# An encoder layer with three token mixers: pooling copies given a greater advance, one multiplication moved from VectorE to GpSimd

## The chip, the cores and the metric

The kernel runs on one core of one Trainium2 chip. The time is that of the device, in microseconds (us), and the median of several runs is what counts. The core's engines are named as the profile names them: PE (TensorE, matmuls; PEld is its weight load), DVE (VectorE), ACT (ScalarE), POOL (GpSimd) and SP (SyncE, which here issues DMAs). Each has its own instruction stream, works through it in order, and waits for the others through semaphores. Matmul results land in PSUM; POOL doesn't touch PSUM in this kernel.

## The reference, cut to what matters

One layer on 512 positions of width 1024, in float32. An RMS norm, one input projection whose columns go to three token mixers and three gates, the mixers, a gated merge, an output projection with residual, and then a SwiGLU feed-forward part (FFN) of inner width 2816.

```python
h = rms_norm(x, norm_mix)
u_pool, u_lru, q, k, v, g_logits = split(h @ w_in)
gates = sigmoid(g_logits + b_gate)
y_pool = pool_mixer(u_pool, w_pool, pool_scale)      # causal means over 2, 4, 8, 16 positions, minus the token, then a 256x256 map per group
y_lru = rglru_mixer(u_lru, ...)                      # short convolution, gates, linear recurrence
y_sb = stick_breaking_attention(q, k, v)             # 8 heads of 128
merged = sum(gates[i] * (y[i] @ w_branch[i]) for i in range(3))
x = x + merged @ w_out
h2 = rms_norm(x, norm_ffn)
x = x + (silu(h2 @ w_ffn_gate) * (h2 @ w_ffn_up)) @ w_ffn_down
```

The RMS norm divides each position by rms = sqrt(mean(x*x) + eps). The kernel keeps 1/rms of the second norm in a tile rb2.

## The kernel before, in words

Activations lie with channels on the 128 partitions and the 512 positions along the free axis. A float32 matmul is made from three passes: each operand is split into a high part in a shorter format and a low part that is the rest (names ending in hi, h and lo, l), and high x high, low x high and high x low are added in PSUM (L309 to L311 in the helper mm3, L318 in the helper product). So each weight tile costs ACT one copy (the high part) and DVE one subtraction (the low part): L141 and L142 in the first stages, L1439 and L1440 in the FFN. Three buffers hold each kind.

Large matrix products are done block-wise with seven products in place of eight (called 11, 12, S2, S1, S3, S4, 22). These need sums of weight blocks, made by DVE (L1421), and partial results copied out of PSUM by ACT (L1492), since the next product is added into the same PSUM bank.

The program is written for a scheduler. It takes the instructions of the five engines in program order and reorders them by priority and by when their inputs would be there; `tc.high_priority(n)` lets what stands in it count as if it had been written n places earlier. EARLY is 300, AHEAD is 200. The streams that come out are fixed before the kernel runs.

*The pooling stage.* Four groups of 256 channels are projected one after the other (pool_chunk, order 1, 0, 3, 2). Each chunk fills two PSUM tiles out of a pool of three (pmm), so a later chunk or branch can start only when a copy has emptied a tile. evac_u makes that copy on ACT (L977); pool_mean then forms the sliding sums on DVE (L985 to L991), and pool_back multiplies by the group's map (tile pps) and scales (L1004, L1005). In between, the tasks of the attention heads are put in: score sigmoids on ACT (L1086, L1087), a scan and a product on DVE (L1090, L1092). After the four chunks come the branch projections (ps_br), which use the same three PSUM tiles.

*The FFN's direct chunks.* The inner width is worked in eleven chunks of 256. The first two (NDIRECT = 2, "direct") are computed in the ordinary way from h2, the second norm's input without 1/rms, since rb2 isn't there yet when they begin. So their results are multiplied by 1/rms afterwards, on both sides of the SiLU. For each half chunk j, with pg and pu the gate and up products in PSUM:

- L1510 (DVE): sg = pg * rb2, which is the SiLU's argument
- L1511 (ACT): sg = SiLU(sg)
- L1512 (DVE): sg = sg * pu
- L1513 (DVE): act = sg * rb2, since pu also lacked its 1/rms

That makes four of each in all. sg lies in a pool with two buffers ("sq2"): the second chunk's two tiles use the buffers of the first chunk's two, and its L1510 may write them only when L1513 has read them. The remaining nine chunks (function seven) use the seven products, with normalised input (tiles B0...). act of both direct chunks is read again only in the last of them, where the operands of the down projection are split.

On POOL itself there is little arithmetic before: constants, and the power function and a few small multiplications of the query scales (L346 to L350, L819); otherwise it issues DMAs, the FFN's only at the down projection (L1552).

Of the kernel before, what the change touches and what calls it, by code (L numbers as in the profile page):

```python
# [11 lines left out]
AF = mybir.ActivationFunctionType  # L12
ALU = mybir.AluOpType
# [13 lines left out]
EARLY = 300  # L27
# [40 lines left out]
def layer_kernel(ctx: ExitStack, tc: tile.TileContext, x, xt, vecs, w_in, w_qkv7, w_gate7, w_pool, w_rg, w_ig,  # L68
                 w_branch, w_br7, w_out, w_fg, w_fu, w_fd, w_fd7, out):
    nc = tc.nc  # L70
    act = nc.scalar.activation
    dve = nc.vector
# [28 lines left out]
    def in_order(ap, b=H):  # L101
        w = ap.ndim == 3
        if b == H:
            return ap.rearrange("p w (b a) -> p w a b" if w else "p (b a) -> p a b", b=b)
        return ap.rearrange("p (c b a) -> p c a b", a=2, b=b)

    def two(ap, b=H):
        w = ap.ndim == 3
        if b == H:
            return ap.rearrange("p w (a b) -> p w a b" if w else "p (a b) -> p a b", b=b)  # L110
        return ap.rearrange("p (c a b) -> p c a b", a=2, b=b)
# [284 lines left out]
    def chan_chunk(key, rhs, nticks=0, pool=None, pair=False):  # L396
        pss = chunk_psum(key, pool, pair)
        for half in range(2):
            half_chunk(pss if type(pss) is list else [pss[:, j, :] for j in range(2)], key, half, rhs,
                       nticks)  # L400
        return pss
# [37 lines left out]
    with ExitStack() as first:  # L439
# [396 lines left out]
        for t in VKQ:  # L836
            ps = {}
# [50 lines left out]
        for cc in range(2):  # L888
# [14 lines left out]
            for nm in ORDER:  # L903
                ps, half, first_, t, ts_, src, ss = plan[nm]
# [18 lines left out]
    def slot(name, dt=F32, shape=(S,)):  # L923
        return sp.tile([P] + list(shape), dt, tag="s", name=name, bufs=NSP - NLD)
# [14 lines left out]
    with ExitStack() as mix:  # L939
# [34 lines left out]

        def evac_u(ps, name):
            u = slot(name)
            act(two(u), in_order(ps), AF.Copy)  # L977
            return u

        def pool_mean(g, j, u):  # L980
# [33 lines left out]
        def pool_chunk(g):  # L1014
            pss = chan_chunk(("pool", g), hn, 1)
            us = [evac_u(pss[j], f"up{g}{j}") for j in range(2)]
            for j in range(2):
                bg.append(lambda j=j, u=us[j]: pool_mean(g, j, u))
            if g != POOL[0]:
                queue_pool_back(POOL[POOL.index(g) - 1])  # L1020
# [199 lines left out]
    with ExitStack() as third:  # L1220
# [42 lines left out]
        for u, nm in BORDER:  # L1263
# [3 lines left out]
            ps = bank[u, z]  # L1267
# [24 lines left out]
    with ExitStack() as ffn:  # L1292
        gp = ffn.enter_context(tc.tile_pool(name="gp", bufs=GBUFS))

        def g4(shape, name, dt=F32):

            return gp.tile([P] + shape, dt, tag="g", name=name)

        def small(name, bufs=1, tag=None, dt=F32):
            return gp.tile([P, S], dt, tag=tag or name, name=name, bufs=bufs)  # L1300
# [5 lines left out]
        rb2 = small("rb2")  # L1306
# [116 lines left out]
        def make_a(upto):  # L1423
            while made[0] < min(upto, len(steps)):
                c, nm = steps[made[0]]
                made[0] += 1
                if (c, nm) == (NDIRECT, "11"):
                    offs.extend(STEPS)
                while made[1] < min(c + 2, DOWN):
                    load_a(made[1])  # L1430
                    made[1] += 1
                sums_a(c, nm)
                A[c, nm] = split_a(raw[c, nm], f"{c}_{nm}")
# [68 lines left out]
        for c in range(NDIRECT):  # L1502
            pg = chan_chunk(("fg", c), h2, 3, fp)
            pu = chan_chunk(("fu", c), h2, 3, fp)
            if c == NDIRECT - 1:
                make_a(3)
            a = g4([2, S], f"act{c}")
            for j in range(2):
                sg = small(f"sg{c}{j}", 2, "sq2")
                dve.tensor_tensor(two(sg), in_order(pg[j]), two(rb2), ALU.mult)  # L1510
                act(sg, sg, AF.Silu)  # L1511
                dve.tensor_tensor(two(sg), two(sg), in_order(pu[j]), ALU.mult)  # L1512
                dve.tensor_tensor(a[:, j, :], sg, rb2, ALU.mult)  # L1513
            acts.append(a)
        tick(len(bg))
        for c in range(NDIRECT, NF // 2):
# [212 lines left out]
```

## Time and profile before

| | |
|---|---|
| median of 3 runs | 874.85 us (873.82 to 877.39) |
| the profiled execution's own time | 873.78 us |
| its span in the profile | 872.0 us |
| PE busy | 859.1 us, 99% |
| DVE busy | 740.8 us, 85% |
| ACT busy | 525.4 us, 60% |
| POOL busy | 90.8 us, 10% |
| granted PE clock | 1.0 throughout |

Times in the profile count from the span's start. A row of the timeline gives the start, the duration, the engine, the line of the program, the operation, what it writes and reads with the shapes, how many such instructions in a row it merges (x2), and in brackets how long the engine had been idle before it and what it then waited for. With x2 the duration is that of both together; successive instructions of one engine overlap by some 0.1 us, so the distance between starts is the pace. A row of the waits names the waiting engine and line, what it waited for, and then the total, the number of times and the longest, in us.

### The profile page before, as it was taken

The page shows a single profiled execution, that of the slowest core. Times are in us where ns is not written, and L with a number is a line of the kernel's source. Part 1 is how long each engine was busy: PE and PEld are TensorE (multiplying, and loading weights), DVE is VectorE, ACT ScalarE, POOL GpSimd, SP SyncE. Part 2 cuts the span into 40 slices and gives each one's busy share as a digit, 9 for nine tenths or more (in the row PEclk, how much of TensorE's full clock was granted, in tenths as well). Part 3 has the DMA queues.
Part 4 walks back from the last instruction along what each step waited for, and adds up shares of the span by engine and source line. Part 5 has one row for each costly group of instructions (what it writes and reads, how often), then busy time and mean ns, then how long its engine had stood idle before and what let it go on. Part 6 is the DMA issues. An engine that isn't in the chain of part 4 may idle for free.

```text
span 872.0 us, 14269 instructions
## 1 busy us (share of the span) xinstructions
PE 859.1 (99%) x5563; PEld 789.4 (91%) x5563; DVE 740.8 (85%) x958; ACT 525.4 (60%) x730; POOL 90.8 (10%) x130
## 2 busy tenths in 40 slices
PE   9999989999999999999999999999999999999998
PEld 7888878888899888889889998889999999999998
DVE  7899797998787699977988796699998888899974
ACT  6655989556956555565665545464555555755642
POOL 1110002132423101000001200000000000031200
PEclk9999999999999999999999999999999999999999
DMA  9586346798592786744636965345543343797913
GB/s 335 160 298 198 97 161 177 206 330 259 174 287 73 228 255 198 225 122 147 216 98 165 201 177 169 98 134 157 144 123 97 104 116 105 232 245 202 195 40 121
DMA packets 116643, 154.08 MB, mean 177 GB/s; under 512 B 8160, under 2 KB 90080, under 8 KB 116576
## 3 DMA queue, kind: packets, MB, share of 16 engines
q1 hardware_dynamic: 103904, 107.30, 38.6%
q0 software_dynamic: 12528, 45.62, 21.8%
q8 instruction: 43, 0.70, 0.3%
q10 hardware_dynamic: 144, 0.26, 0.1%
q14 instruction: 24, 0.20, 0.1%
HBM read 132.71 MB, written 18.87 MB: 174 GB/s over the span
## 4 chain that ended last, share of the span: by engine, by line
PE 77%; DVE 11%; ACT 6%; DMA 3%; issue 2%; SPq 0%; ACTq 0%; DVEq 0%
PE ps_y L318 10%; PE ps_x L318 8%; PE ps_q L831 7%; PE ps_dy L1648 6%; PE ps_dx L1648 5%; DVE wlo L142 3%; PE ps_br L309 3%; PE ps_br L310 3%; PE ps_br L311 3%; PE ps_bY L1274 2%; PE ps_gate L734 2%; PE ps_gy L318 2%; PE ps_bX L1274 2%; PE ps_gx L318 2%; ACT whi L141 2%
## 5 line engine op out<-in xcount | busy, mean ns | idle before, releaser
L141 ACT ACTIVATE whi<-raw 128x1024 fp32r<-128x1024 f32 x69 | 72.8, 1055 | 77.4 <-PE ps_out L310 16.2
L142 DVE TENSOR_TENSOR wlo<-raw,whi 128x1024 fp32r<-128x1024 f32 x69 | 84.3, 1222 | 21.8 <-ACT whi L141 21.3
L142 DVE TENSOR_TENSOR wlo<-qw,whi 128x1024 fp32r<-128x1024 f32 x48 | 58.5, 1222 | 18.2 <-ACT whi L141 18.0
L141 ACT ACTIVATE whi<-qw 128x1024 fp32r<-128x1024 f32 x48 | 50.5, 1054 | 28.9 <-PE ps_q L831 14.8
L1439 ACT ACTIVATE wh_S<-w_S 128x1024 fp32r<-128x1024 f32 x36 | 38.1, 1062 | 32.9 <-PE ps_y L318 19.5
L1552 POOL DMA_DIRECT2D dw<-in_w_down_dram x20 | 16.9, 862 | 306.6 <-DMA dw<-in_w_down_dram 264.3
L1440 DVE TENSOR_TENSOR wl_S<-w_S,wh_S 128x1024 fp32r<-128x1024 f32 x36 | 43.8, 1221 | 3.8 <-ACT wh_S L1439 3.8
L1439 ACT ACTIVATE wh<-w 128x1024 fp32r<-128x1024 f32 x27 | 28.6, 1058 | 27.3 <-issue 9.1
L1440 DVE TENSOR_TENSOR wl<-w,wh 128x1024 fp32r<-128x1024 f32 x27 | 33.0, 1221 | 8.4 <-ACT wh L1439 8.4
L1439 ACT ACTIVATE whdS<-dw 128x1024 fp32r<-128x1024 f32 x20 | 21.2, 1060 | 20.9 <-PE ps_dy L1648 10.6
L1440 DVE TENSOR_TENSOR wldS<-dw,whdS 128x1024 fp32r<-128x1024 f32 x20 | 24.3, 1222 | 5.3 <-ACT whdS L1439 5.3
L1090 DVE TENSOR_TENSOR_SCAN E<-K,ahead 128x512 f32<-128x512 f32 (+3 forms) x32 | 25.4, 815 | 3.9 <-ACT K L1086 3.9
L311 PE MATMUL ps_gate<-HH,wlo 128*128 128x512 f32 x64 | 24.4, 381 | 2.2 <-DVE wlo L142 2.2
L309 PE MATMUL ps_br<-yHH,whi 128*128 128x512 f32 x64 | 24.6, 385 | 1.4 <-ACT up L977 1.4
L309 PE MATMUL ps_lru<-HH,whi 128*128 128x512 f32 x64 | 24.6, 384 | 0.0
L309 PE MATMUL ps_br<-yph,whi 128*128 128x512 f32 x64 | 24.5, 383 | 0.0
L309 PE MATMUL ps_pool<-HH,whi 128*128 128x512 f32 x64 | 24.5, 383 | 0.0
L309 PE MATMUL ps_gate<-HH,whi 128*128 128x512 f32 x64 | 24.4, 381 | 0.0
L310 PE MATMUL ps_lru<-HL,whi 128*128 128x512 f32 x64 | 24.3, 379 | 0.0
L311 PE MATMUL ps_lru<-HH,wlo 128*128 128x512 f32 x64 | 24.3, 379 | 0.0
L310 PE MATMUL ps_gate<-HL,whi 128*128 128x512 f32 x64 | 24.3, 379 | 0.0
L310 PE MATMUL ps_pool<-HL,whi 128*128 128x512 f32 x64 | 24.3, 379 | 0.0
(737 smaller groups left out, 3445.1 us busy)
## 6 DMA issues: line engine op xcount, KB each, us to landing
raw<-in_w_in_dram SPq DMA_DIRECT2D x31, 512.0 KB, 5.4
qw<-in_w_qkv_dram SPq DMA_DIRECT2D x24, 512.0 KB, 7.1
dw<-in_w_down_dram POOLq DMA_DIRECT2D x20, 512.0 KB, 8.7
w<-in_w_ffn_gate_dram SPq DMA_DIRECT2D x36, 256.0 KB, 3.5
w<-in_w_ffn_up_dram SPq DMA_DIRECT2D x36, 256.0 KB, 4.2
raw<-in_w_branch_dram SPq DMA_DIRECT2D x16, 512.0 KB, 3.8
qw<-in_w_qkv_dram POOLq DMA_DIRECT2D x12, 512.0 KB, 8.0
qd<-r POOLq DMA_DIRECT2D x12, 512.0 KB, 7.6
```

Source lines behind the costliest of these rows:

```text
L141: act(hi, raw, AF.Copy)
L142: dve.tensor_tensor(lo, raw, hi.bitcast(F32), ALU.subtract)
L309: nc.tensor.matmul(ps, lh, rh, start=start, stop=False, skip_group_check=skip)
L310: nc.tensor.matmul(ps, lh, rl, start=False, stop=False, skip_group_check=skip)
L311: nc.tensor.matmul(ps, ll, rh, start=False, stop=stop, skip_group_check=skip)
L318: nc.tensor.matmul(o, a_[a][:, w, k, :], il2(b_[b][:, k, :]), start=first and n == k == 0, stop=last and n == 2 and k == 3, skip_group_che ...
L831: nc.tensor.matmul(ps[:, a, :], b_[:, k, ts_], il(a_[:, kk, :]), start=first and n == k == 0, stop=n == 2 and k == 3, skip_group_check=True)
L1090: dve.tensor_tensor_scan(E[:, c0:c0 + n][:, ::-1], K[:, c0 + 1:c0 + n + 1][:, ::-1], ahead[:, S - n:][:, ::-1], 0.0, ALU.mult, ALU.add)
L1274: nc.tensor.matmul(o, ah[x_][:, w, k, :], il2(b[k][y_]), start=first_ and n == k == 0, stop=n == 2 and k == 3, skip_group_check=True)
L1439: act(h, src, AF.Copy)
L1440: dve.tensor_tensor(l, src, h.bitcast(F32), ALU.subtract)
L1648: nc.tensor.matmul(o, a_[a][:, w, k0 + k, :], il2(b_[b][:, k, :]), start=first and i == k == 0, stop=last and i == 2 and k == nk - 1, skip ...
```

## The change

Two independent edits. evac_u's copy is put under high_priority(EARLY), so that the scheduler treats it as if it stood 300 places earlier. And L1513, the second multiplication by 1/rms of the two direct chunks, is issued on POOL instead of DVE. What is computed stays the same. The new line in evac_u shifts the line numbers after it by one: L1513 of the program before is L1514 in the changed one.

```diff
         def evac_u(ps, name):
             u = slot(name)
-            act(two(u), in_order(ps), AF.Copy)
+            with tc.high_priority(EARLY):
+                act(two(u), in_order(ps), AF.Copy)
             return u
...
                 dve.tensor_tensor(two(sg), in_order(pg[j]), two(rb2), ALU.mult)
                 act(sg, sg, AF.Silu)
                 dve.tensor_tensor(two(sg), two(sg), in_order(pu[j]), ALU.mult)
-                dve.tensor_tensor(a[:, j, :], sg, rb2, ALU.mult)
+                nc.gpsimd.tensor_tensor(a[:, j, :], sg, rb2, ALU.mult)
             acts.append(a)
```

## Prediction

> **What bounds the kernel now.** I read the page first (busy shares, then the chain that ended last), after it who waited for whom on the matrix engine (PE), and then the stretches of the two edits.
>
> ```profile
> span 872.0 us, 14269 instructions
> PE 859.1 (99%) x5563; PEld 789.4 (91%) x5563; DVE 740.8 (85%) x958; ACT 525.4 (60%) x730; POOL 90.8 (10%) x130
> ...
> PE 77%; DVE 11%; ACT 6%; DMA 3%; issue 2%; SPq 0%; ACTq 0%; DVEq 0%
> ...
> PE ps_br L309 <- ACT up L977: 1.4, 1, 1.4
> ...
> PE ps_x L318 <- DVE wl_S L1440: 0.8, 1, 0.8
> ...
> PE ps_x L318 <- ACT wh_S L1439: 0.2, 1, 0.2
> ```
>
> PE is busy for 859.1 of 872.0 us, so nothing off PE can bring more than it takes away from PE's waits. Three waits lie where the change works: 1.4 us for a copy of pooling products (L977), and 0.8 + 0.2 us for weights that VectorE (DVE) and ScalarE (ACT) prepare just after the direct chunks. The other waits are elsewhere.
>
> ```profile
> 580.00:600.00 20.00, 20.00 (x119) 18.23 (x118) 20.00 (x23) 12.13 (x14) 0.00 (x0) 1.00 0.80 211
> 600.00:620.00 20.00, 19.07 (x168) 18.68 (x167) 19.38 (x20) 11.31 (x15) 0.00 (x0) 1.00 0.47 132
> 620.00:640.00 20.00, 20.00 (x181) 20.00 (x180) 18.22 (x17) 11.69 (x14) 0.00 (x0) 1.00 0.38 107
> ```
>
> These are windows (stretch, length, then busy time of PE, weight loads, DVE, ACT and POOL, the granted clock, DMA share, GB/s). The products from 594 on are those of the first chunk computed with seven products (11, 12, S2, S1, S3, S4, 22, here the first to the seventh). Around the direct chunks' end DVE is full (20.00 of 20 us) and PE loses 0.93 us in 600 to 620; by 620 to 640 DVE has caught up and PE is full. The clock is 1.00, so PE's pace is not in question.
>
> **Edit 1, the pooling copies.** A greater priority can only change the order in which ACT is given its work. I compared the instruction streams of both builds: of eight copies, only the second chunk's two move, ahead of one sigmoid (L1087, 384 columns). PE's, DVE's, POOL's and SP's streams are untouched by it.
>
> ```profile
> 315.18 0.59 ACT L1087 ACTIVATE A<-z,qrs 128x384 f32<-128x384 f32 x1
> 315.64 1.10 ACT L977 ACTIVATE up<-ps_pool 128x512 f32<-128x512 f32 x2
> ...
> 316.73 0.69 DVE L1092 TENSOR_TENSOR A<-A,E 128x512 f32<-128x512 f32 x1
> ...
> 350.23 1.11 ACT L977 ACTIVATE up<-ps_pool 128x512 f32<-128x512 f32 x2
> ...
> 350.90 0.48 PE L309 MATMUL ps_br<-yHH,whi 128*128 128x512 f32 x1 [1.45 <-ACT up L977]
> ```
>
> The wait of 1.45 us belongs to the fourth chunk's copies at 350.23, and those stay behind the same instructions. The second chunk's copies come 0.46 us earlier (315.64 - 315.18) and no PE wait hangs on them. The sigmoid starts after the two copies, at 315.18 + 1.10 = 316.28, and ends at 316.87, where DVE's product with A started at 316.73: at most 0.15 us late. What hides that is PE's queue of other matmuls: the view of waits names no wait of PE for this product. Uncovered it would cost its 0.15 us. I take 0; the ends are -1.45 (the wait goes) and +0.15.
>
> **Edit 2, what DVE loses and gains.** Four multiplications of L1513 leave DVE. Their results, act, are next read in the last chunk, so nobody is in a hurry for them. POOL's queue is empty there (0.00 busy from 580 to 640), and behind the four stand only its loads for the down projection. But their input sg has two buffers, and the second chunk's L1510 reuses them: DVE now waits for GpSimd (POOL) there. Behind that wait are queued on DVE the sum for the fourth product, the low parts wl_S of the third and fourth, and L1512; ACT's SiLU (L1511) waits for L1510, PE for the low parts.
>
> ```profile
> 590.17 1.29 DVE L1512 TENSOR_TENSOR sg<-sg,ps_fu 128x512 f32<-128x512 f32 x2
> 591.37 1.29 DVE L1513 TENSOR_TENSOR act<-sg,rb 128x512 f32<-128x512 f32 x2
> 592.57 1.23 DVE L1440 TENSOR_TENSOR wl<-w,wh 128x1024 fp32r<-128x1024 f32 x1
> 593.71 1.23 DVE L1421 TENSOR_TENSOR w_S<-w,w 128x1024 f32<-128x1024 f32 x1
> 594.84 0.69 DVE L1510 TENSOR_TENSOR sg<-ps_fg,rb 128x512 f32<-128x512 f32 x1
> ...
> 602.56 2.36 DVE L1440 TENSOR_TENSOR wl_S<-w_S,wh_S 128x1024 fp32r<-128x1024 f32 x2 [0.54 <-ACT wh_S L1439]
> ...
> 596.76 1.07 ACT L1439 ACTIVATE wh_S<-w_S 128x1024 fp32r<-128x1024 f32 x1 [0.50 <-DVE w_S L1421]
> 597.96 0.63 ACT L1511 ACTIVATE sg<-sg 128x512 f32<-128x512 f32 x1
> 598.50 0.58 ACT L1492 ACTIVATE tx<-ps_y 128x512 f32<-128x512 f32 x1
> ...
> 594.22 0.27 PE L318 MATMUL ps_y<-B011h,wh 128*128 128x256 f32 x1
> ...
> 602.58 0.38 PE L318 MATMUL ps_x<-B0T1h,wh_S 128*128 128x256 f32 x1 [0.16 <-ACT wh_S L1439]
> 603.84 0.38 PE L318 MATMUL ps_x<-B0T1h,wl_S 128*128 128x256 f32 x1 [0.77 <-DVE wl_S L1440]
> 606.56 2.68 PE ps_y L318 x24
> ```
>
> Successive starts give the pace: 1.14 us for 1024 columns on DVE (592.57 to 593.71), 0.60 for 512 ((591.37 - 590.17) / 2). So the removal frees 4 x 0.60 = 2.4 us of a full engine. If POOL's work cost DVE nothing, DVE would have five 1024-column and four 512-column operations between 591.37 and the fourth product's wl_S in the new order: 591.37 + 5 x 1.14 + 4 x 0.60 = 599.5 instead of 602.56. Both waits, 0.16 + 0.77 = 0.93 us, would go.
>
> **What POOL's multiplication takes.** No multiplication of this width stands in the trace.
>
> ```profile
> L952 POOL MEMSET K<- 128x513 f32 x2 | 1.0, 528 | 0.0
> ...
> 263.88 1.22 DVE L217 TENSOR_TENSOR qs<-qw,qw 128x1024 f32<-128x1024 f32 x1
> 265.01 1.26 DVE L142 TENSOR_TENSOR wlo<-qw,whi 128x1024 fp32r<-128x1024 f32 x1
> ...
> 264.74 0.45 POOL L347 TENSOR_TENSOR qrs<-qrs 128x32 f32<-128x32 f32 x1
> 265.27 1.11 POOL L348 TENSOR_TENSOR qrs<-qrs,qss 128x32 f32<-128x32 f32 x1
> 266.48 0.21 POOL L349 TENSOR_SCALAR qrs<-qrs 128x32 f32<-128x32 f32 x1
> 266.77 0.25 POOL L350 TENSOR_TENSOR qrs<-qrs 128x32 f32<-128x32 f32 x1
> ```
>
> Low end: POOL writes 513 columns in 528 ns, so 0.53. High end: 0.25 us for 32 columns (L350, DVE idle) times 16 = 4.0, which counts the start-up sixteen times. Nearest in width is the memset; two operands read in turn at its pace make 2 x 528 ns = 1.06, and with about 0.1 of start-up I take 1.15. The Trainium skill (GPSIMD Engine Reference, section 3.1) gives 2.6 cycles an element at 1.2 GHz for two inputs, an estimate of 1.11 us here; no run so far shows it.
>
> The same rows show POOL held up by DVE: L348 starts at 265.27 and ends at 266.38, right behind L142's end (265.01 + 1.26 = 266.27); L347 ends at 265.19, right behind L217's (265.10). Both DVE operations read two operands from SBUF. So POOL waits for the running one and gets in before the next. What DVE suffers from a 512-column POOL instruction these 32-column ones can't show. I take it that the two alternate.
>
> **The walk through the new order.** The new streams also put wh_S of the fourth product ahead of the copy tx on ACT, and two sums ahead of the fifth product's wl_S on DVE. The first multiplication runs from 590.9, behind the first L1512, to 592.05; DVE's next operation, due at 591.37, loses 0.7. Three 1024-column operations bring DVE to 595.45. Then the second multiplication gets in, beside the first L1510, which reads PSUM and only one operand from SBUF; it frees sg's second buffer at 596.7, so the second L1510 ends at 597.3 and the sum for the fourth product at 598.5 (were it to get in earlier, 0.5 later). ACT makes wh_S from that sum (598.6 to 599.6: its row has 1.07, of which some 0.1 overlaps the next start) and only then tx, 0.58, until 600.15. The third product accumulates in the bank that tx is copied from, so it starts at 600.17, not at 594.22 + 2 x 2.68 = 599.58 (594.22 is PE's first product in the trace, each is 24 matmuls in 2.68): 0.6 us lost. The third multiplication then holds DVE by 0.65; the fourth product's wl_S is ready at 602.7, in time. The fifth's, behind two sums (602.6, 603.7), is made from 604.9 and ready at 606.1, where PE, which starts that product at 600.17 + 2 x 2.68 = 605.5, reads it with its third matmul, 0.2 later: 0.4 lost. After that DVE is no later than it was before, with one sum already done that used to come after. Sum: +0.6 + 0.4 - 0.93 = +0.07, so 873.85 against the profiled execution's 873.78 (span 872.0 and 1.78 around it). The median of the runs shown is 874.85, 1.07 above that execution; I forecast 874.9.
>
> **Rivals.** *A, slower: POOL's multiplication is long and holds DVE throughout.* Two of them stand before the third product and one before the fourth, so each further 1 us costs about 3 us of PE. From 1.15 + (4.4 - 0.1) / 3 = 2.6 us on, the kernel is over 0.5% slower; at 3.0, 874.9 + 3 x 1.85 = about 880.5. At the high end, 4.0, it is 883.5. For it: L350's 0.25 for 32 columns. Against: the memset's pace, and L348's 0.11 us behind the end of L142. The Trainium skill (SBUF — State Buffer, section SBUF: two separate sides) has DVE operations with two SBUF inputs and POOL instructions share a lock: whichever starts first keeps it for its whole instruction.
>
> ```profile
> 219.47 2.50 POOL L346 TENSOR_TENSOR rsqq<-ssq,mhalf 128x8 f32<-128x8 f32 x1 [2.70 <-DVE ssq L799]
> ...
> 220.36 1.23 DVE L142 TENSOR_TENSOR wlo<-qw,whi 128x1024 fp32r<-128x1024 f32 x1
> ```
>
> By that rule this L142 would have waited until 221.97; it ran inside the POOL instruction at its usual 1.23 us, so the trace bears out only the half in which POOL waits.
>
> *B, a little faster: DVE isn't held by POOL at all*, or the multiplication is at its low end of 0.53, where four of them hold DVE for less than the 2.4 us freed. Then the 0.93 us goes and nothing comes: 874.85 - 0.93 = 873.9. The undisturbed L142 above speaks for it; that instruction has only 8 columns to read, which speaks against.
>
> *C, the advance does what it says:* the copies before the 1.45 us wait move after all, 874.9 - 1.45 = 873.4. Against: the fourth chunk's copies keep their place.
>
> **How the numbers follow.** Forecast 0.55, B 0.28, A 0.13 (0.10 of it beyond 0.5%), C 0.04. A difference of 0.5%, 4.4 us, is about what a measurement of this kernel can tell from no change. No case reaches 4.4 us of gain, since the waits in reach sum to 1.45 + 0.93 = 2.4; I leave 0.02 for it. Range: below B and C and the lowest run shown less B's gain, 873.82 - 0.93 = 872.9, rounded out to 872.6 (C ends inside); above, a multiplication of 1.76 us (16 times L348's 0.11) gives 874.9 + 1.8 = 876.7, and the runs shown reach 2.5 above their median, so 878.6.
>
> **What would show it.** Right: four POOL multiplications near 1.15 us between 590 and 602, longer where a DVE operation runs; DVE's sums or wl_S late by about one of them; the PE wait moved from the fourth to the third and fifth product, some 1 us in all; the 1.45 us wait at 350 unchanged. B: DVE operations at their usual 1.14 pace and no PE wait between 594 and 613. Wrong: PE waits over 3 us there, a POOL multiplication above 2.6 us, or L1510 waiting several us for POOL; also any change outside these two stretches.

## The result, and the profile after

The changed kernel takes 877.51 us in the median (22 runs, 875.11 to 880.02), the kernel before 875.86 us in as many runs (873.71 to 877.39). The ratio is 1.0021 with a 95% interval of 1.0012 to 1.0029: slower by 1.8 us, between 1.1 and 2.5. It lies within 0.5% and within the forecast range. The forecast itself, no loss worth the name, missed these 1.8 us; as a time, 874.9, it was 2.6 us too low, since the median of the kernel before also came out 1.0 us higher over 22 runs than over the three shown ahead of the prediction.

The page's busy shares and PE's waits over the whole changed kernel (waiting engine and line, what it waited for, total us, times, longest). Line numbers after L977 are one higher than before.

```profile
span 877.3 us, 14273 instructions
PE 861.9 (98%) x5563; PEld 791.1 (90%) x5563; DVE 742.5 (85%) x954; ACT 524.9 (60%) x730; POOL 98.7 (11%) x134
...
PE ps_y L318 <- ACT tx L1493: 2.0, 2, 1.3
...
PE ps_br L309 <- ACT up L978: 1.5, 1, 1.5
PE pq L1054 <- DMA at<-qd: 1.4, 1, 1.4
...
PE ps_y L318 <- DVE wl_S L1441: 0.2, 1, 0.2
```

The two waits of the fourth product (0.8 + 0.2 us before) are gone, and 2.0 + 0.2 us have come at the third and fifth. The wait of ps_br for the pooling copy is where it was. DVE did four instructions fewer and was busy longer (742.5 us after 740.8). The wait for at<-qd is new here, but it isn't the change's: it ends at 304 us, ahead of the first instructions that the change moves (the second chunk's copies, at 319 us here), and the profile of the multiplication's move alone (experiment 2) doesn't have it and is as slow. The span, 5.3 us above the one profiled before, also holds a stretch of lower clock (0.98 from 60 to 130 us) that the profiles of the kernel before and of experiments 2 and 4 don't have. So the spans are not compared here, but the windows, the waits and one stretch that is measured further down.

The same three windows as before the change:

```profile
580.00:600.00 20.00, 20.00 (x103) 17.75 (x102) 20.00 (x19) 10.44 (x11) 3.48 (x2) 1.00 0.85 230
600.00:620.00 20.00, 17.79 (x154) 17.22 (x154) 19.86 (x19) 10.77 (x15) 3.51 (x2) 1.00 0.37 107
620.00:640.00 20.00, 20.00 (x182) 20.00 (x180) 18.17 (x18) 11.63 (x14) 0.00 (x0) 1.00 0.50 139
```

PE now loses 2.21 us between 600 and 620 where it lost 0.93: 1.3 us more. DVE is still full.

That is not yet all that PE loses. PE's matmuls come in the same order in all the profiles of this case, so their starts can be compared one by one. The first matmul of the first seven-product chunk is at 594.22 before the change (its row stands in the prediction); the first of the next chunk follows here, and then both rows of the changed kernel:

```profile
614.44 0.28 PE L318 MATMUL ps_y<-B011h,wh 128*128 128x256 f32 x1
```

```profile
598.02 0.27 PE L318 MATMUL ps_y<-B011h,wh 128*128 128x256 f32 x1
...
619.79 0.28 PE L318 MATMUL ps_y<-B011h,wh 128*128 128x256 f32 x1
```

The chunk takes 614.44 - 594.22 = 20.22 us before and 619.79 - 598.02 = 21.77 us after: 1.55 us more. From 310 us on the same matmuls are 3.8 us later in the changed kernel's profile than in the one before, up to this chunk, and 5.35 us later from its end to the end of the kernel. So PE gains or loses nothing else there. The 1.55 us fit the measured 1.8 (1.1 to 2.5). They are more than the waits say, because a wait costs PE more than its row: before the matmul of 602.58, for instance, PE is idle for 0.16 us, and yet that matmul and the next one together come 0.43 us later than at PE's pace, as the first matmul behind a wait takes 0.38 us in place of 0.28. That is 0.27 us on top of each wait.

Rows of the changed kernel's timeline, POOL first, then DVE, ACT and PE (this execution is 3.8 us later here than the one shown before):

```profile
594.90 3.48 POOL L1514 TENSOR_TENSOR act<-sg,rb 128x512 f32<-128x512 f32 x2 [88.95 <-DMA w<-in_w_ffn_up_dram]
604.83 3.51 POOL L1514 TENSOR_TENSOR act<-sg,rb 128x512 f32<-128x512 f32 x2 [6.45 <-ACT tx L1493]
...
593.99 1.28 DVE L1513 TENSOR_TENSOR sg<-sg,ps_fu 128x512 f32<-128x512 f32 x2
595.18 2.07 DVE L1422 TENSOR_TENSOR w_S<-w,w 128x1024 f32<-128x1024 f32 x1
597.18 2.29 DVE L1441 TENSOR_TENSOR wl<-w,wh 128x1024 fp32r<-128x1024 f32 x1
599.39 1.21 DVE L1422 TENSOR_TENSOR w_S<-w,w_S 128x1024 f32<-128x1024 f32 x1
600.52 1.28 DVE L1511 TENSOR_TENSOR sg<-ps_fg,rb 128x512 f32<-128x512 f32 x2
...
605.21 1.99 DVE L1441 TENSOR_TENSOR wl_S<-w_S,wh_S 128x1024 fp32r<-128x1024 f32 x1
607.23 2.19 DVE L1422 TENSOR_TENSOR w_S<-w,w_S 128x1024 f32<-128x1024 f32 x1
...
601.24 0.64 ACT L1512 ACTIVATE sg<-sg 128x512 f32<-128x512 f32 x1 [7.30 <-DVE sg L1511]
...
604.19 0.59 ACT L1493 ACTIVATE tx<-ps_y 128x512 f32<-128x512 f32 x1
...
609.54 1.06 ACT L1440 ACTIVATE wh_S<-w_S 128x1024 fp32r<-128x1024 f32 x1 [3.80 <-DVE w_S L1422]
610.50 0.58 ACT L1493 ACTIVATE tx<-ps_y 128x512 f32<-128x512 f32 x1
...
604.84 0.38 PE L318 MATMUL ps_y<-B0T2h,wh_S 128*128 128x256 f32 x1 [1.29 <-ACT tx L1493]
611.13 0.38 PE L318 MATMUL ps_y<-B0T3h,wh_S 128*128 128x256 f32 x1 [0.67 <-ACT tx L1493]
611.87 0.38 PE L318 MATMUL ps_y<-B0T3h,wl_S 128*128 128x256 f32 x1 [0.25 <-DVE wl_S L1441]
```

This is how a blocked operation looks here: it isn't idle, it is long. The sum at 595.18 has its usual 1.22 us of work and a duration of 2.07; if it was held first and then worked at its usual pace, it began work at 595.18 + 2.07 - 1.22 = 596.03, which is 1.13 us after POOL's first multiplication began (594.90). Then it is POOL's turn to wait: the first multiplication takes 1.27 us, the second 2.25. The second ends at 598.38 (594.90 + 3.48), and the next DVE operation, 2.29 us long, begins work at 597.18 + 2.29 - 1.22 = 598.25. The same happens again at 605. That POOL and DVE take turns is borne out by the ends: POOL's second multiplication ends 1.13 us after the DVE operation at 595.18 does (597.25), and the DVE operation after it 1.09 us behind that. Four multiplications lengthen DVE's operations by (2.07 + 2.29 + 1.99 + 2.19) - 4 x 1.22 = 3.7 us, and 2.4 us were saved. L1511 at 600.52 waits for nobody: POOL had read both buffers by 598.4.

### The profile page after: what moved, and what is told of

The parts are those of the page before. It is cut to its first block, busy times and chain, and to the rows that moved or that the text cites. A ratio compares the mean times of both kernels' runs of the same rounds, so it can differ in the third digit from the quotient of the medians.

```text
span 877.3 us, 14273 instructions
## 1 busy us (share of the span) xinstructions
PE 861.9 (98%) x5563; PEld 791.1 (90%) x5563; DVE 742.5 (85%) x954; ACT 524.9 (60%) x730; POOL 98.7 (11%) x134
## 4 chain that ended last, share of the span: by engine, by line
PE 77%; DVE 10%; ACT 6%; DMA 4%; issue 2%; SPq 0%; POOL 0%; ACTq 0%; DVEq 0%; POOLq 0%
PE ps_y L318 10%; PE ps_x L318 8%; PE ps_q L831 6%; PE ps_dy L1649 6%; PE ps_dx L1649 5%; PE ps_br L309 3%; PE ps_br L310 3%; PE ps_br L311 3%; PE ps_bY L1275 2%; PE ps_gate L734 2%; DVE wlo L142 2%; DMA qw<-in_w_gate_dram 2%; ACT whi L141 2%; PE ps_bX L1275 2%; PE ps_gy L318 2%
## 5 line engine op out<-in xcount | busy, mean ns | idle before, releaser
L142 DVE TENSOR_TENSOR wlo<-raw,whi 128x1024 fp32r<-128x1024 f32 x69 | 84.5, 1224 | 22.0 <-ACT whi L141 21.4
L142 DVE TENSOR_TENSOR wlo<-qw,whi 128x1024 fp32r<-128x1024 f32 x48 | 58.5, 1223 | 18.5 <-ACT whi L141 18.4
L310 PE MATMUL ps_br<-ypl,whi 128*128 128x512 f32 x64 | 24.3, 379 | 0.0
```

The source lines that it names most:

```text
L142: dve.tensor_tensor(lo, raw, hi.bitcast(F32), ALU.subtract)
L310: nc.tensor.matmul(ps, lh, rl, start=False, stop=False, skip_group_check=skip)
```

## The experiments

All were timed against the kernel before, on the same chip as their neighbours. In diffs, lines are those of the kernel before.

**1. The copies alone (copies_only).** Only the first hunk of the change.

> Only the copies out of PSUM get the greater advance; the multiplication stays on DVE. Theory L (the shared SBUF access: POOL's multiplications hold DVE, and nothing else of the change matters): ratio 1.000, within 0.5 us of before; the wait of 1.4 to 1.5 us of ps_br for the copy is still there, and PE's waits for weights at the first seven-product chunk are those of before (0.9 us). Rival E (the copies cause part of the 1.8 us): 1 us or more slower, with a new PE wait between 295 and 350 us, such as the 1.4 us for at<-qd in the profile of the changed kernel.

Ratio 1.0004, 0.9993 to 1.0014: no difference that shows, and at most 1.2 us. PE's waits between 285 and 640 us in its profile:

```profile
PE ps_br L309 <- ACT up L978: 1.4, 1, 1.4
PE ps_x L318 <- DVE wl_S L1441: 0.8, 1, 0.8
PE pq L1054 <- POOL K L952: 0.5, 1, 0.5
...
PE ps_x L318 <- ACT wh_S L1440: 0.2, 1, 0.2
...
PE pq L1054 <- DMA at<-qd: 0.2, 1, 0.2
```

The waits of the pooling copy and at the first seven-product chunk are those of before. The two of pq are new, but they end at 304 and 305 us, and the first instructions that this edit moves, the second chunk's copies, start at 319 us. From 310 us to the end PE's matmuls keep the same distance to those of before, within 0.02 us. So rival E (the copies cost something) and the prediction's rival C (the advance takes the 1.4 us away) both fall.

**2. The multiplication alone (mult_only).** Only the second hunk.

> Only the multiplication moves to POOL; the copies stay as before. Theory L: all of the loss is here: 1.3 to 1.8 us slower (ratio 1.0015 to 1.002), PE waits at the first seven-product chunk 2.2 us in sum in place of 0.9, at the third and fifth product, and three to four 1024-column DVE operations stretched from 1.22 to about 2 us. Rival E: half of that or less.

Ratio 1.0022, 1.0012 to 1.0033, as for the whole change. Its waits over the same stretch:

```profile
PE ps_y L318 <- ACT tx L1492: 1.9, 2, 1.3
PE ps_br L309 <- ACT up L977: 1.4, 1, 1.4
...
PE ps_y L318 <- DVE wl_S L1440: 0.2, 1, 0.2
```

The first seven-product chunk takes 21.74 us. The loss is all in this edit.

**3. No second multiplication at all (no_mult).** This leaves the four multiplications out, and DVE and ACT then issue in the very order of the changed kernel.

```diff
-                dve.tensor_tensor(two(sg), two(sg), in_order(pu[j]), ALU.mult)
-                dve.tensor_tensor(a[:, j, :], sg, rb2, ALU.mult)
+                dve.tensor_tensor(two(a[:, j, :]), two(sg), in_order(pu[j]), ALU.mult)
```

> The second multiplication by 1/rms of the direct chunks is left out altogether: L1512 writes act. DVE's and ACT's instructions then come in the same order as in the changed kernel, with no arithmetic on POOL there. Theory L: the 0.93 us of waits at the first seven-product chunk go and none comes: 0.9 us faster (ratio 0.999). Rival O (the new order costs by itself, with wh_S of the fourth product ahead of the copy tx and two sums ahead of the fifth product's wl_S): PE waits at the third and fifth product remain, 1 to 2 us, and the time is that of before or up to 1 us above.

Ratio 0.9989, 0.9979 to 0.9999. PE has no wait at the first seven-product chunk. The chunk's first matmul and the next chunk's, then its DVE at the places that are stretched above:

```profile
595.86 0.27 PE L318 MATMUL ps_y<-B011h,wh 128*128 128x256 f32 x1
...
614.62 0.28 PE L318 MATMUL ps_y<-B011h,wh 128*128 128x256 f32 x1
```

```profile
593.01 1.23 DVE L1421 TENSOR_TENSOR w_S<-w,w 128x1024 f32<-128x1024 f32 x1
594.15 1.23 DVE L1440 TENSOR_TENSOR wl<-w,wh 128x1024 fp32r<-128x1024 f32 x1
...
601.15 1.22 DVE L1440 TENSOR_TENSOR wl_S<-w_S,wh_S 128x1024 fp32r<-128x1024 f32 x1
602.41 1.22 DVE L1421 TENSOR_TENSOR w_S<-w,w_S 128x1024 f32<-128x1024 f32 x1
```

So the new order alone costs nothing (rival O falls). The chunk takes 18.76 us, seven products at 2.68, and that is 1.46 less than before: the 0.93 us of waits and 0.27 us with each of the two. The runs give 1.0 us (0.1 to 1.8), which agrees with either. What turns that gain into a loss is POOL's work itself.

**4. POOL without anyone waiting for it (pool_inplace).** L1512 writes into act, sg is free at once, and POOL multiplies act in place.

```diff
-                dve.tensor_tensor(two(sg), two(sg), in_order(pu[j]), ALU.mult)
-                dve.tensor_tensor(a[:, j, :], sg, rb2, ALU.mult)
+                dve.tensor_tensor(two(a[:, j, :]), two(sg), in_order(pu[j]), ALU.mult)
+                nc.gpsimd.tensor_tensor(a[:, j, :], a[:, j, :], rb2, ALU.mult)
```

> L1512 writes its product into act and frees sg, and POOL multiplies act by 1/rms in place: the same orders as without the multiplication, but POOL works and L1510 need not wait for POOL. Theory L: as slow as the multiplication alone on POOL, 1.3 to 1.8 us slower than before, with the same stretched DVE operations. Rival W (L1510's wait for POOL costs the time): 0.9 us faster than before.

Ratio 1.0018, 1.0005 to 1.0030: as slow as experiment 2. No instruction of DVE in this stretch depends on POOL, and four are stretched beside it all the same (2.07, 2.29, 1.93 and 2.18 us). The first two:

```profile
591.64 3.48 POOL L1513 TENSOR_TENSOR act<-act,rb 128x512 f32<-128x512 f32 x2 [89.25 <-DMA w<-in_w_ffn_gate_dram]
...
591.93 2.07 DVE L1421 TENSOR_TENSOR w_S<-w,w 128x1024 f32<-128x1024 f32 x1
593.92 2.29 DVE L1440 TENSOR_TENSOR wl<-w,wh 128x1024 fp32r<-128x1024 f32 x1
```

Rival W (the semaphore wait of L1510) falls.

**5. The price doubled (pool_twice).** POOL does each of the four multiplications of the second hunk twice; the copies are as before.

```diff
-                dve.tensor_tensor(a[:, j, :], sg, rb2, ALU.mult)
+                for _ in range(2):
+                    nc.gpsimd.tensor_tensor(a[:, j, :], sg, rb2, ALU.mult)
```

> POOL does each of the four multiplications twice, with the same result, so that it works eight times. Theory L (each multiplication holds DVE for its own 1.1 us or so, taking turns): two more stand before the third product and two before the fifth, PE waits at the first seven-product chunk of 5 to 6 us in sum, 4 to 5 us slower than before (ratio about 1.005), and up to eight stretched DVE operations of some 2.1 to 2.3 us. Rival (DVE loses only the first encounter, or POOL's work is hidden once it has started): no more than 2 us slower than before.

Ratio 1.0048, 1.0029 to 1.0066: 4.2 us slower. The waits at the first seven-product chunk, and DVE from the first multiplication on:

```profile
PE ps_y L318 <- ACT tx L1492: 2.8, 1, 2.8
PE ps_y L318 <- DVE wl_S L1440: 1.8, 1, 1.8
```

```profile
593.65 7.93 POOL L1514 TENSOR_TENSOR act<-sg,rb 128x512 f32<-128x512 f32 x4 [89.32 <-DMA w<-in_w_ffn_up_dram]
...
593.93 2.07 DVE L1421 TENSOR_TENSOR w_S<-w,w 128x1024 f32<-128x1024 f32 x1
595.93 2.29 DVE L1440 TENSOR_TENSOR wl<-w,wh 128x1024 fp32r<-128x1024 f32 x1
598.14 2.30 DVE L1421 TENSOR_TENSOR w_S<-w,w_S 128x1024 f32<-128x1024 f32 x1
600.36 0.68 DVE L1510 TENSOR_TENSOR sg<-ps_fg,rb 128x512 f32<-128x512 f32 x1
601.61 0.69 DVE L1510 TENSOR_TENSOR sg<-ps_fg,rb 128x512 f32<-128x512 f32 x1 [0.57 <-POOL act L1514]
```

These are strict turns: each of POOL's instructions goes between two of DVE's. DVE's third held operation ends at 600.44 (598.14 + 2.30), and POOL's four end at 601.58, 1.14 us later, as after one turn of POOL. L1510, which reads only one operand from SBUF, keeps its 0.68 us inside POOL's stretch (593.65 to 601.58). Now the buffers bind too, 0.57 us. Seven DVE operations are stretched, not eight, since one of POOL's falls beside L1510. The waits, 4.6 us, were expected at 5 to 6.

In this profile the chunk takes 25.52 us, 5.3 more than before, and not all of that is waiting. Between the two waits PE's granted clock was down for some 3 us:

```profile
606.60:609.70 3.10, 3.10 (x17) 3.10 (x16) 3.07 (x2) 0.00 (x0) 3.03 (x2) 0.50 0.01 2
```

It was 0.50 there, and matmuls came every 0.21 us in place of 0.11, which costs some 1.6 us. Whether the other three runs of this kernel had that too isn't known.

**6. POOL that only writes (pool_memset), and that reads one operand (pool_one_in).** Each ran once, so only the traces are read. Both leave the multiplication by 1/rms out; in its place POOL writes a constant into act, or multiplies act by a constant.

```diff
+                nc.gpsimd.memset(a[:, j, :], 1.0)                                   # pool_memset
+                nc.gpsimd.tensor_scalar(a[:, j, :], a[:, j, :], 0.5, None, ALU.mult)  # pool_one_in
```

> The multiplication is left out; in its place POOL writes a constant into the same 512 columns of act, reading nothing from SBUF. Same order on DVE and ACT as with the multiplication left out. If POOL's reading is what holds DVE: DVE's 1024-column operations keep 1.22 us beside it and PE waits at the first seven-product chunk are 0. If any POOL access to SBUF holds it: the operations beside it take 1.5 to 1.75 us.

> The multiplication by 1/rms is left out; in its place POOL multiplies act by a constant, with one operand read from SBUF. Theory L: it holds DVE for its own duration; if it reads at the pace at which POOL writes (0.53 us for 513 columns), the 1024-column DVE operations beside it take 1.5 to 1.9 us, four of them, and PE waits at the first seven-product chunk stay below 0.5 us since the four hold less than the 2.4 us freed. Rival (only two operands read by POOL make the conflict): DVE keeps 1.22 us.

The memsets and the DVE operations beside them, then the same of pool_one_in:

```profile
593.72 0.99 POOL L1513 MEMSET act<- 128x512 f32 x2 [88.92 <-DMA w<-in_w_ffn_gate_dram]
...
594.04 1.23 DVE L1421 TENSOR_TENSOR w_S<-w,w 128x1024 f32<-128x1024 f32 x1
```

```profile
593.40 3.03 POOL L1513 TENSOR_SCALAR act<-act 128x512 f32<-128x512 f32 x2 [89.37 <-DMA w<-in_w_ffn_up_dram]
...
593.67 1.42 DVE L1421 TENSOR_TENSOR w_S<-w,w 128x1024 f32<-128x1024 f32 x1
595.01 1.62 DVE L1440 TENSOR_TENSOR wl<-w,wh 128x1024 fp32r<-128x1024 f32 x1
```

A POOL instruction that only writes lets DVE's two-operand operation run at 1.23 us. One that reads a single operand lengthens it by 0.2 and 0.4 us (the second pair, not shown, by 0.04 and 0.29; 0.3 to 0.7 had been expected). The first began at 593.40 and let DVE begin at 593.67 + 1.42 - 1.22 = 593.87, after 0.47 us. So, as far as these three instructions show, it is POOL's reading that holds DVE, and not for the instruction's own length (1.5 us each): Theory L had that part wrong. No wait of PE is named at the first seven-product chunk in either; in pool_one_in the chunk is still 0.3 us longer than without POOL's work (19.08 us).

**7. The multiplication kept on DVE, but later (dve_spread).** L1512 writes into act as in experiment 3, and one multiplication in place follows each of the chunks 3 to 6.

```diff
             seven(c)
+            if 3 <= c < 7:
+                t = acts[(c - 3) // 2][:, (c - 3) % 2, :]
+                tc.keep_in_program_order(dve.tensor_tensor(t, t, rb2, ALU.mult))
```

> The multiplication stays on DVE but is moved in time: L1512 writes into act, and the four multiplications in place are pinned one each behind the chunks 3, 4, 5 and 6, where DVE has some 1 to 1.8 us of slack for each product and each costs 0.60. Theory L: the 0.93 us of PE waits at the first seven-product chunk go as without the multiplication and none comes later: 0.9 us faster than before (ratio 0.999), with act still complete. Rival (DVE has no slack later, the work only moves): PE waits of up to 0.6 us each at the chunks 4 to 7, and the time of before.

Ratio 0.9990, 0.9982 to 0.9999: 0.9 us faster than before, and faster than the changed kernel. From 560 to 700 us PE waits for nothing in its profile, and the first seven-product chunk takes 18.76 us as in experiment 3; the window over its four multiplications:

```profile
604.00:700.00 96.00, 96.00 (x862) 96.00 (x861) 88.49 (x83) 54.76 (x67) 0.00 (x0) 1.00 0.41 116
```

## Why the prediction was right or wrong

**What bounds the kernel, and edit 1:** right. The edit was put at 0, and from 310 us on it moves PE by no more than 0.02 us. The streams said that the fourth chunk's copies don't move, and the 1.4 us wait stayed (experiment 1).

**What DVE gains:** right in kind: both waits go when the multiplication is gone or moved away from the full stretch (experiments 3 and 7, 0.9 to 1.0 us by the runs). The size, 0.93 us, was read off the waits' rows; by the starts of the matmuls it is 1.46.

**What POOL's multiplication takes:** right to about a tenth. 1.15 us were assumed; DVE was held for 1.13 where it can be read off, near twice the memset's 0.53, and the instruction itself took 1.27 us at its shortest. The Trainium skill's 2.6 cycles an element (GPSIMD Engine Reference, section 3.1), an estimate of 1.11 us, agrees with the hold and is 0.16 below the instruction. Rival A's multiplication of 2.6 us and more didn't come: the longest, 2.27 us, includes its wait for DVE.

**That the two alternate:** right, and shown (experiments 4 and 5). Rival B, that DVE isn't held, falls. For the one trace row cited for B, the L142 that ran undisturbed inside a POOL instruction, experiment 6 suggests a reason: DVE is held while POOL reads, and that instruction has only eight columns to read. No run tests it. The Trainium skill's rule (SBUF — State Buffer, section SBUF: two separate sides), that the lock is kept for the whole instruction, nearly holds for the two-operand multiplication, 1.13 us of 1.27; for the one-operand one it doesn't, 0.47 us held of 1.5.

**The walk through the new order:** this is the step that failed. The terms were the right ones, a loss at the third product and one at the fifth, but both were too small. The walk let the second multiplication in only at L1510, where half of it would be free, so that DVE reached the first L1510 with 0.7 us lost. POOL in fact got in after the very next operation (a case that the walk puts in brackets, at 0.5 us), and 0.85 + 1.07 = 1.92 us were lost by then. ACT works without a break from the SiLU of that L1510 (601.24 in the changed kernel) to tx, so all of it reaches tx. In experiment 3 tx is done 0.48 us before the third product is due; 1.92 - 0.48 = 1.44, and the third product starts 1.46 us late (604.84 in place of 598.02 + 2 x 2.68 = 603.38). The walk had 0.6.

After the third multiplication the walk left out the fourth, which stands in POOL's queue right behind it. That one holds the sum at 607.23 by 1.0 us. ACT waits for this sum before wh_S (609.54), behind which stands the tx of the fifth product (610.50), and DVE makes the fifth's wl_S two operations later; so the fifth product waited 0.67 us for tx and 0.25 for wl_S, 0.9 in place of 0.4.

Together that is 2.2 us of waits against the 1.0 forecast. The walk counted its losses by the starts of matmuls, and so counted the chunk loses 21.77 - 18.76 = 3.0 us; less the 1.46 that went, +1.55 in place of +0.07. Both terms follow from the assumption made, turns, had it been applied to POOL's queue as strictly as to DVE's.

**The range:** that it holds the measured time is not owed to the walk. Its upper end was set for a longer multiplication (1.76 us) and for the spread of the runs, and its sum is off: 876.7 + 2.5 is 879.2, not 878.6. The measured 877.51 lies inside either.

**The price per microsecond in rival A:** about 3 us of PE for each further 1 us of POOL was somewhat high, as far as experiment 5 can stand for it: with twice as many multiplications (1.1 us each) the waits grew from 2.2 to 4.6 us, by 2.4, where the rule gives 3.3. That experiment has more multiplications and not longer ones.

**What is left open:** the 1.55 us at the chunk and the measured 1.8 (1.1 to 2.5) leave nothing that has to be explained. The profiles differ by more than that ahead of 310 us, where the change moves nothing. One example is the wait of ps_gy for ACT's gx: 1.3 us in experiment 2, 0.3 in experiment 4, 0.6 in experiment 5. With one profile of each kernel it can't be told from chance.

## What to carry to other kernels

Moving an operation off a full engine helps only if the other engine's work doesn't hold the first one up: here each 0.60 us saved on DVE cost 0.8 to 1.1 us of it, because DVE's next operation also read two operands from SBUF. Before moving work to POOL, look at what DVE runs beside it; and before either, ask when the result is needed. Here the cheapest place was the same engine, some 45 to 90 us later. And price a wait by when the work behind it starts, not by the idle time alone: here each wait of PE cost 0.27 us more than its row.

## What the runs showed of the hardware that had not been expected

A multiplication by a constant on POOL, with one operand read, takes about 1.5 us for 512 columns, longer than the multiplication of two tensors at its shortest (1.27 us), yet it holds DVE for less than 0.5 us (0.47 where it can be read off). A memset of the same width takes 0.53 and holds nothing.

In experiment 5 PE's granted clock fell to 0.50 for 3.1 us, 1.3 us after PE had waited for 2.8 us. At this chunk no other profile of this case shows it; what set it off isn't shown.
